# A two-layer encoder trunk on one core: block products in the FFN's input projection

## The chip, the core and the metric

The kernel runs on one core of a Trainium2 chip. The core has five engines that run their own instruction queues in order: TensorE (PE), which multiplies 128-row tiles and writes only to the accumulator memory PSUM; VectorE (DVE); ScalarE (ACT); GpSimd (POOL); and SyncE (SP), which here only issues DMAs. Data lie in SBUF, 128 partitions wide. The metric is device time in microseconds of one execution, as the median of several.

## The reference

Input x is 256 tokens by 1024. Two layers, each with three residual sub-layers; all is float32. The FFN is the part that the change touches:

```python
def _swiglu(h, w_in, w_out):
    gate, up = jnp.split(h @ w_in, 2, axis=-1)      # w_in 1024 x 5632
    return (jax.nn.silu(gate) * up) @ w_out         # w_out 2816 x 1024

for l in range(2):
    h = _swiglu(_rmsnorm(x, g[0]), ffn_w_in[l, 0], ffn_w_out[l, 0])
    x = x + 0.5 * _rmsnorm(h, g[1])
    h = _mixer(_rmsnorm(x, g[2]), ...)              # attention heads and mLSTM heads
    x = x + _rmsnorm(h, g[3])
    h = _swiglu(_rmsnorm(x, g[4]), ffn_w_in[l, 1], ffn_w_out[l, 1])
    x = x + 0.5 * _rmsnorm(h, g[5])
```

## The kernel before

**Six phases** follow one another: FFN, mixer, FFN, FFN, mixer, FFN. There are two token tiles of 128 (t = 0, 1), and the dimension D = 1024 is cut into two halves (kh = 0, 1) of four blocks of 128 each (k).

**Precision in two parts.** Matmuls run on a rounded float32 form, so each operand is split into a high part and a low remainder, and each block product is three matmuls into the same PSUM bank: high by high, high by low, low by high (`mm3`, L401 to L403). Tokens are the stationary operand (128x128), weights the moving one (128x512).

**Weights** come as pieces of 1 MB (128 x 2048): `begin_piece` issues the DMA on SP's queue into one of three raw buffers (`wr`), and each of its two halves (128 x 1024) is cast to its high part on ACT (L288, `wh`) and subtracted to its low part on DVE (L289, `wl`). The halves live in two pools of seven (`wl`, `wh`); while `lend` is set, three halves of every ten are taken from a third pool (`k4`, six tiles, two for each half). The cast and the split of a half wait until an older half has been used up by PE.

**An FFN phase** goes over the 2816 hidden columns in 11 chunks of 256 (gate and up, so 512 columns of w_in). For a chunk, two pieces of w_in are used: `in_piece` makes 12 matmuls for each token tile and half of D, 48 in all, into one bank for each token tile (tags `pin` and `ptr`, two banks each, in turns). `ffn_hidden` then makes silu(gate) * up: an ACT instruction (`func`, L266) and one on DVE (L528). `ffn_planes` turns the result: ACT copies it to 16-bit planes (L535), a transposing DMA on SP's queue follows (L537), DVE copies it back to float32 (L539, `hT`), and `ffn_hilo` splits it (L550 on ACT, L551 on DVE) into four buffers of each of `hh` and `hl`, two chunks' worth. `out_part` multiplies that by a piece of w_out (24 matmuls for both token tiles) into four banks that stay for the phase (`bk`). The output projection of a chunk runs behind the input projection of a later one (`DEFER`). The last chunk (`in_turned`, L610 and L615, `ffn_turned`) computes the transposed product directly, so that it needs no transposing DMA, and the outputs of chunks 8, 9 and 10 come last, token tile 0 ahead of 1, so that the norms of the next phase can begin. The first FFN phase starts with a chunk of its own, written out by hand (`first_chunk`), in which L371 splits the first two pieces.

**Around a phase**, `postnorm` and `prenorm_half` scale, add, transpose (L427) and split the tokens (L431 to L433) into tiles with the tag `both`, four buffers: two for the tokens of a phase, two more that the mixer uses for its output.

**Order.** Instructions are written in program order, and a scheduler that simulates the engines when the program is built fixes each engine's order and gives out buffers as they come free in its simulation. Only around the ends of phases (from "ending" to "running") is PE's order that of the program. `turns` and `after` add single orderings by hand. Small tiles of 128 x 512 (`h`, `planes`, `turned`, `hT` and others) share five buffers by the tag `ev`.

Of the kernel before, what the change touches and what calls it, by code (L numbers as in the profile page):

```python
# [17 lines left out]
F32 = mybir.dt.float32  # L18
F32R = mybir.dt.float32r
# [6 lines left out]
P = 128  # L26
# [10 lines left out]
DEFER = 3  # L37
TURN = 10
# [21 lines left out]
def _pack(inp):  # L60
# [9 lines left out]
    def ffn(at, l, f):  # L70
        a = w_in[l, f].reshape(2, 4, P, 2, NC_FF, 256)
        a = a.transpose(4, 0, 2, 1, 3, 5).reshape(NC_FF, 2, P, 2048)
        b = w_out[l, f].reshape(NC_FF, 2, P, D).transpose(0, 2, 1, 3).reshape(NC_FF, P, 2048)
        order = [a[0, 0], a[0, 1]]
        for c in range(1, NC_FF):
            order += [a[c, 0], a[c, 1], b[c - 1]]
        for piece in order + [b[NC_FF - 1]]:
            w[at] = piece
            at += 1
# [52 lines left out]
class _Trunk:  # L132
# [16 lines left out]
    for _n in ("nat", "ra", "rb", "rv", "tmp", "y", "so", "xg", "h", "planes", "turned", "hT"):  # L149
        TAGS[_n] = ("ev", 5)  # L150
# [32 lines left out]
    def constants_mix(self):  # L183
# [53 lines left out]
        self.qk = self.ded.tile([P, 4, S], F32, name="qk")  # L237
        self.qd = self.ded.tile([P, 2, CH], F32, name="qd")
        self.vx = self.ded.tile([P, NT, 4, P + 1], F32, name="vx")
        self.wt = self.ded.tile([P, NT, 2, 2, P], F32, name="wt")  # L240
# [36 lines left out]
    def begin_piece(self):  # L277

        nc, i = self.nc, self.piece_at
# [3 lines left out]
        js = iter(range(2))  # L283

        def part():
            j = next(js)
            lo, hi = self.half_tiles(i, j)
            ia = nc.scalar.activation(hi, raw[:, j], AF.Copy)  # L288
            iv = nc.vector.tensor_tensor(lo, raw[:, j], hi.bitcast(F32), op=ALU.subtract)  # L289
            for oa, ov in self.turns.pop(0) if self.turns else ():  # L290
                self.after(ia, [oa] if oa else [])
                self.after(iv, [ov] if ov else [])
            return hi, lo

        return part

    def half_tiles(self, i, j):
# [3 lines left out]
        return [pools[n].tile([P, 1024], F32R, tag=pools[n + 1], name=f"{nm}_{i}_{j}") for n, nm in ((0, "wl"), (2, "wh"))]  # L301
# [31 lines left out]
    def first_chunk(self, pins, xT):  # L333
# [30 lines left out]
        def H(i, k):  # L364
            if k % 2 == 0:
                lo[i, k // 2], hi[i, k // 2] = self.half_tiles(i, k // 2)
            self.cast = nc.scalar.activation(self.cols({k // 2: (hi[i, k // 2], lo[i, k // 2])}, k)[0], raw(i, k), AF.Copy)
# [162 lines left out]
    def ffn_planes(self, h):  # L530


        nc = self.nc
        planes = self.t2("planes", (P, 2, 512), U16)
        nc.scalar.activation(planes, h.rearrange("p t j -> p (t j)").bitcast(U16).rearrange("p (n u) -> p u n", u=2), AF.Copy)  # L535
# [3 lines left out]
        nc.vector.tensor_copy(hT.rearrange("p b n -> p (b n)").bitcast(U16).rearrange("p (n u) -> p u n", u=2),  # L539
                              turned.rearrange("p (u b) n -> p u (b n)", u=2))  # L540
        ops = [self.ffn_operand() for _ in range(NT)]
        for t in range(NT):
            self.ffn_hilo(hT[:, 2 * t:2 * t + 2], *ops[t])
        return [[tuple(v[:, k] for v in ops[t]) for k in range(2)] for t in range(NT)]
# [42 lines left out]
    def ffn(self, pre, gi_post):  # L587
# [30 lines left out]
        po, pend = None, []  # L618
        if not xT:
# [12 lines left out]
            h = self.t2("h", (P, NT, 256))  # L632
            for t in range(NT):
                self.ffn_hidden(pins[t], r[t], h[:, t])
            h = self.ffn_planes(h)
            begin = 1
        else:
# [17 lines left out]
            pend = [(0, self.ffn_planes(h), self.piece())]  # L655
# [6 lines left out]
            h = self.ffn_planes(h)  # L662
            begin = 2
        for c in range(begin, NC_FF):
            ws = [self.piece(), self.piece()]
            pend.append((c - 1, h, self.piece()))
            if c == 3:
                g = self.load_gpost(gi_post)
                yield "middle"
            if c < TURN:  # L670
                pins = [self.bank_pin() if c % 2 else self.bank_tr() for _ in range(NT)]
# [3 lines left out]
                h = self.t2("h", (P, NT, 256))  # L675
                for t in range(NT):
                    self.ffn_hidden(pins[t], r[t], h[:, t])
                h = self.ffn_planes(h)
            else:
                rows, both = self.token_scales(r), list(self.both)  # L680
                banks = [[self.bank_pin() for _ in range(2)], [self.bank_tr() for _ in range(2)]]
                in_turned(banks, ws, both)
                break
            if len(pend) == DEFER - 1:
                if po is None:
                    po = [[self.bank_bk() for _ in range(2)] for _ in range(NT)]
                cc, hc, wo = pend.pop(0)
                for t in range(NT):
                    out_part(cc, t, hc, wo)

        yield "ending"
        pend.append((c, self.ffn_turned(banks, rows), self.piece()))
        for p in pend:
            out_part(p[0], 0, *p[1:])
        yield "done", po[0], g
        for p in pend[:-1]:
            out_part(p[0], 1, *p[1:])
        yield "next"
        out_part(pend[-1][0], 1, *pend[-1][1:])
# [58 lines left out]
class _Mixer:  # L758


    def __init__(self, tr, pre, l):
        self.tr, self.l = tr, l
        self.xT, self.r = pre
        self.yT = [[None, None] for _ in range(NT)]
        self.conved = None
        self.rot, self.qkT, self.so, self.p = [], [], [], {}
        self.aT, self.lsum, self.hn, self.y = [None] * NT, [None] * NT, [None] * NT, [None] * NT
# [145 lines left out]
    def conv_silu(self):  # L913
        tr, conv = self.tr, self.conved
        tr.func(tr.qk, conv, AF.Silu)
        self.q, self.kT = tr.qk[:, 0:2, :], tr.qk[:, 2:4, :]
# [119 lines left out]
    def intra_weights(self):  # L1036
# [9 lines left out]
        for t in range(NT):  # L1046
            for hh in range(2):
                eE = self.eE[t].rearrange("p (a b j) -> p a b j", a=2, b=2)
                self.stt(tr.wt[:, t, :, hh, :], pss[hh][:, t], 0.125, eE[:, :, hh, :], op0=ALU.mult, op1=ALU.mult)
# [116 lines left out]
    def numerators(self, t):  # L1166
# [3 lines left out]
        for pr in range(2):  # L1170
            for hh in range(2):
                mm(num[hh][:, pr, :], tr.wt[:, t, pr, hh, :], tr.vx[:, t, 2 * pr + hh, :],
# [84 lines left out]
```

## Time and profile before

| | us |
|---|---|
| median of 3 runs | 961.61 (961.54 to 962.01) |
| the profiled execution | 962.02 |
| its span | 960.2 |
| PE, ACT, DVE busy | 952.8, 571.2, 638.7 |
| first FFN phase, until the next norm's first transposes | 0 to 185 |
| first mixer | 185 to 293 |
| FFN phases two and three | 293 to 477 to 659 |
| second mixer, last FFN | 659 to 766 to 960 |

The bounds of the phases are the starts of the prenorm's transposes on PE (L427) in the chain that ended last. A few per cent of the matmul records can be missing. In a row of a group stand the line, engine, operation, output and inputs by name, how many, then busy time in all and the mean of one in ns, then the idle time of the engine just before them and what released it. A row of windows has the stretch, then for PE, PEld (weight loads), DVE, ACT and POOL the busy time with the count, then the clock, the DMA share and GB/s; with a line given it has only that line's engine. A row of the timeline has start, length, engine, line, operation and, where several were merged, their count. The length of a matmul in the trace is more than the time until the next one starts, as matmuls are pipelined.

### The profile page before, as it was taken

To read this page: it belongs to the slowest core of one execution; us is meant where nothing else is said; L and a number is where in the kernel's file an instruction comes from. 1 tells how busy PE (TensorE), PEld (TensorE's weight loads), DVE (VectorE), ACT (ScalarE), POOL (GpSimd) and SP (SyncE) were. 2 spreads that over 40 slices of the span, in tenths; PEclk is the share of its full clock that TensorE was granted. 3 is DMA by queue.
4 is the path that set the end of the run, shared out by engine and by line. 5 is a ranking of instruction groups with operands and counts; after the bars stand their busy time and mean duration, and the time that the engine had idled before them with its cause. 6 is when DMAs were issued, how large, how long until landed. Compare 5 with 4: busy or idle time off the path is not lost.

```text
span 960.2 us, 12037 instructions
## 1 busy us (share of the span) xinstructions
PE 952.8 (99%) x4523; PEld 788.9 (82%) x4523; DVE 638.7 (67%) x945; ACT 571.2 (59%) x937; POOL 29.5 (3%) x55
## 2 busy tenths in 40 slices
PE   9999999999999999999999999999999999999997
PEld 7888888888888888888888888888888888888885
DVE  6765655689867766555687555566988676755553
ACT  8755554577856655454476555555778466555542
POOL 2000000000010000000000000000001000000000
PEclk9999999999999999999999999999999999999999
DMA  8996656236352975676458666653454257765621
GB/s 317 328 288 202 225 193 219 105 132 241 116 192 91 299 245 193 218 247 176 154 189 283 206 225 208 196 187 128 172 202 174 90 182 256 272 205 192 225 72 44
DMA packets 69879, 189.32 MB, mean 197 GB/s; under 512 B 45274, under 2 KB 46426, under 8 KB 49086
## 3 DMA queue, kind: packets, MB, share of 16 engines
q1 hardware_dynamic: 69246, 187.95, 58.0%
q8 instruction: 35, 0.57, 0.2%
q10 hardware_dynamic: 576, 0.61, 0.2%
q14 instruction: 22, 0.18, 0.1%
HBM read 177.01 MB, written 1.05 MB: 185 GB/s over the span
## 4 chain that ended last, share of the span: by engine, by line
PE 97%; DVE 1%; DMA 1%; ACT 0%; issue 0%; POOLq 0%; DVEq 0%; ACTq 0%
PE pin L401 13%; PE pin L402 13%; PE pin L403 13%; PE bk L401 10%; PE bk L402 10%; PE bk L403 10%; PE ptr L402 6%; PE ptr L403 6%; PE ptr L401 6%; PE pin L610 1%; PE ptr L610 1%; PE ptr L879 1%; PE ptr L427 1%; DMA wr<-in_w_dram 1%; PE bk L1094 1%; PE ptr L615 1%
## 5 line engine op out<-in xcount | busy, mean ns | idle before, releaser
L289 DVE TENSOR_TENSOR wl<-wr,wh 128x1024 fp32r<-128x1024 f32 x324 | 389.2, 1221 | 180.4 <-ACT wh L288 174.4
L288 ACT ACTIVATE wh<-wr 128x1024 fp32r<-128x1024 f32 x324 | 333.9, 1055 | 171.2 <-DMA wr<-in_w_dram 44.1
L401 PE MATMUL pin<-wh,both 128*128 128x512 f32 x560 | 221.2, 396 | 0.0
L403 PE MATMUL pin<-wh,both 128*128 128x512 f32 x560 | 218.3, 390 | 0.0
L402 PE MATMUL pin<-wl,both 128*128 128x512 f32 x560 | 218.2, 390 | 0.0
L401 PE MATMUL bk<-wh,hh 128*128 128x512 f32 x352 | 137.4, 390 | 0.1
L402 PE MATMUL bk<-wl,hh 128*128 128x512 f32 x352 | 137.0, 389 | 0.0
L403 PE MATMUL bk<-wh,hl 128*128 128x512 f32 x352 | 136.9, 389 | 0.0
L403 PEld LDWEIGHTS pin<-wh,both 128*128 128x128 f32 x560 | 105.1, 188 | 22.3
L401 PEld LDWEIGHTS pin<-wh,both 128*128 128x128 f32 x560 | 105.3, 188 | 22.0 <-issue 0.7
L402 PEld LDWEIGHTS pin<-wl,both 128*128 128x128 f32 x560 | 105.3, 188 | 20.6
L403 PE MATMUL ptr<-wh,both 128*128 128x512 f32 x256 | 99.4, 389 | 0.0
L402 PE MATMUL ptr<-wl,both 128*128 128x512 f32 x256 | 99.4, 389 | 0.0
L401 PE MATMUL ptr<-wh,both 128*128 128x512 f32 x256 | 98.9, 389 | 0.0
L401 PEld LDWEIGHTS bk<-wh,hh 128*128 128x128 f32 x352 | 66.1, 188 | 14.0 <-ACT hh L550 0.5
L403 PEld LDWEIGHTS bk<-wh,hl 128*128 128x128 f32 x352 | 66.1, 188 | 13.7
L402 PEld LDWEIGHTS bk<-wl,hh 128*128 128x128 f32 x352 | 66.1, 188 | 13.5
L539 DVE COPY hT<-turned 128x1024 uint16<-128x1024 uint16 x40 | 30.3, 757 | 41.9 <-DMA turned<-planes 41.5
L401 PEld LDWEIGHTS ptr<-wh,both 128*128 128x128 f32 x256 | 48.1, 188 | 10.0
L402 PEld LDWEIGHTS ptr<-wl,both 128*128 128x128 f32 x256 | 48.1, 188 | 10.0
L550 ACT ACTIVATE hh<-hT 128x256 fp32r<-128x256 f32 x80 | 28.9, 409 | 46.0 <-DVE hT L539 46.0
L403 PEld LDWEIGHTS ptr<-wh,both 128*128 128x128 f32 x256 | 48.1, 188 | 9.9
(210 smaller groups left out, 891.9 us busy)
## 6 DMA issues: line engine op xcount, KB each, us to landing
wr<-in_w_dram SPq DMA_DIRECT2D x162, 1024.0 KB, 5.2
gpost<-in_gpost_dram SPq DMA_DIRECT2D x6, 512.0 KB, 6.3
wr<-in_w_dram SPq DMA_DIRECT2D x2, 512.0 KB, 6.1
wr<-in_w_dram SPq DMA_DIRECT2D x3, 256.0 KB, 4.3
x<-in_x_dram SPq DMA_DIRECT2D x3, 256.0 KB, 4.4
turned<-planes SPq DMA_TRANSPOSE x40, 4.4
out_dram<-x SPq DMA_DIRECT2D x2, 256.0 KB, 2.1
x<-in_x_dram SPq DMA_DIRECT2D x2, 128.0 KB, 3.0
```

The costliest lines, as they stand in the source:

```text
L288: ia = nc.scalar.activation(hi, raw[:, j], AF.Copy)
L289: iv = nc.vector.tensor_tensor(lo, raw[:, j], hi.bitcast(F32), op=ALU.subtract)
L401: mm(ps, xh, wh, start=start, stop=False)
L402: mm(ps, xh, wl, start=False, stop=False)
L403: mm(ps, xl, wh, start=False, stop=stop)
L427: nc.tensor.transpose(ptr[:, k, :], x[:, (4 * hf + k) * P:(4 * hf + k + 1) * P], self.ident)
L539: nc.vector.tensor_copy(hT.rearrange("p b n -> p (b n)").bitcast(U16).rearrange("p (n u) -> p u n", u=2), turned.rearrange("p (u b) n -> p ...
L550: self.nc.scalar.activation(hh, h, AF.Copy)
L610: self.nc.tensor.matmul(b, self.cols(w[kh], k)[0][:, c], both[kh][:, k].rearrange("p i t -> p (i t)"), start=kh == 0 and k == 0, stop=Fals ...
L615: self.nc.tensor.matmul(b[:, 0:NT * P], self.cols(w[kh], k)[1][:, c], both[kh][:, k, 0:NT].rearrange("p i t -> p (i t)"), start=False, sto ...
L879: self.T(ptr[:, b, :], a[:, b * P:(b + 1) * P], self.tr.ident)
L1094: self.mm(pcs[c][:, h, :], self.qkT[0][rows, h0 + h, t * P:(t + 1) * P], self.qkT[1][rows, h0 + h, 0:nk], start=True, stop=True)
```

## The change

Write the tokens as four blocks X(kh, t) and the weights of two neighbouring chunks as four blocks W(kh, g), where g is gate or up, now for both chunks at once (512 columns each). Each of the four results (t, g) is a sum over kh of two block products, eight in all. Strassen's form in Winograd's arrangement gets them from seven products (P1 to P7) of sums of blocks. In each FFN phase chunks 4, 5 and chunks 8, 9 are done so.

- The phase is a list of steps (`STEPS`): I for a chunk's input projection as before, P for a pair, O for a chunk's output projection. The pieces in memory follow that order; a pair has four pieces, one for each block.
- `pair_tokens` makes, once a phase, four sums of token blocks from their high and low parts, and splits them again, into two more `both` tiles.
- `pair_blocks` splits seven blocks of weights in place of four: three blocks as loaded (P1, P2, P3) and four sums, which take four additions of whole blocks (128 x 2048, in two DVE instructions each). Three of the sums follow one another in a tile of their own (`wide`), the fourth lies in the raw buffer of its operand.
- `pair` runs the seven products into four banks, where P2, P3 and P4 accumulate on the bank of an earlier one, and adds the rest with DVE in tiles u, v and h0 of 512 columns.
- For all chunks the copy `hT` after the transposing DMA goes from DVE to ACT.
- The mixer's tiles `qk` and `wt` lie in the `wide` tile, which the mixer takes while no pair uses it.

```diff
-DEFER = 3
-TURN = 10
+STEPS = "I2 O0 I3 O1 P4 O2 I6 O3 I7 O4 O5 P8 O6 O7 I10".split()
+END = (8, 9, 10)
...
+    def fetch(self):
+        nc, i = self.nc, self.piece_at
+        self.piece_at += 1
+        raw = self.raw_tile(i)
+        self.load = nc.sync.dma_start(raw.rearrange("p a b -> p (a b)"), self.a["w"][i])
+        return raw
+
+    def halved(self, raw):
+        nc = self.nc
+        lo, hi = self.half_tiles()
+        ia = nc.scalar.activation(hi, raw, AF.Copy)
+        iv = nc.vector.tensor_tensor(lo, raw, hi.bitcast(F32), op=ALU.subtract)
...
+        return hi, lo
+
+    def wide(self):
+        return self.k4.tile([P, 2, 1024], F32, tag="wide", bufs=1, name=self.name("wide"))
+
+    def pair_blocks(self):
+        def split(raw):
+            return [self.halved(raw[:, j]) for j in range(2)]
+
+        def add(out, a, b):
+            for j in range(2):
+                self.nc.vector.tensor_tensor(out[:, j], a[:, j], b[:, j], op=ALU.add)
+
+        b11, b12 = self.fetch(), self.fetch()
+        w = {"P1": split(b11)}
+        run = self.wide()
+        add(run, b11, b12)
+        w["P5"] = split(run)
+        b22 = self.fetch()
+        add(run, run, b22)
+        w["P6"] = split(run)
+        add(b12, b12, b22)
+        w["P7"] = split(b12)
+        b21 = self.fetch()
+        w["P2"] = split(b21)
+        w["P3"] = split(b22)
+        add(run, run, b21)
+        w["P4"] = split(run)
+        return w
+
+    def pair_tokens(self, both):
+        tt = self.nc.vector.tensor_tensor
+        tiles = [self.tr.tile([P, 4, 2 * NT, P], F32R, tag="both", name=self.name("both")) for _ in range(2)]
...
+        s1 = apart((0, 1), (1, 1))
+        x1 = split(0, s1)
+        s2 = less((0, 0), s1)
+        x2 = split(1, s2)
+        x4 = split(3, less((1, 0), s2))
+        return x1, x2, split(2, apart((0, 0), (0, 1))), x4
...
         nc.sync.dma_start_transpose(turned, planes.rearrange("p u n -> p (u n)"))
-        hT = self.t2("hT", (P, 4, P))
-        nc.vector.tensor_copy(hT.rearrange("p b n -> p (b n)").bitcast(U16).rearrange("p (n u) -> p u n", u=2),
-                              turned.rearrange("p (u b) n -> p u (b n)", u=2))
+        hT = self.t2("hT", (P, 2, 2, P))
+        nc.scalar.activation(hT.rearrange("p a b n -> p (a b n)").bitcast(U16).rearrange("p (n u) -> p u n", u=2),
+                             turned.rearrange("p (u b) n -> p u (b n)", u=2), AF.Copy)
+        return hT
...
+        def product(b, x, w, new):
+            for k in range(4):
+                for n, (st, mv) in enumerate(((x[0], 0), (x[0], 1), (x[1], 0))):
+                    self.nc.tensor.matmul(b, st[:, k, :], self.cols(w, k)[mv], start=new and k == n == 0,
+                                          stop=k == 3 and n == 2, skip_group_check=True)
+
+        def pair(c):
+            tt, stt = self.nc.vector.tensor_tensor, self.nc.vector.scalar_tensor_tensor
+            w = self.pair_blocks()
+            b1, b2, b3, b4 = self.bank_pin(), self.bank_pin(), self.bank_tr(), self.bank_tr()
+            s1, s2, s3, s4 = sums
+            product(b1, xT[0][0], w["P1"], True)
+            p1 = self.t2("p1")
+            self.nc.scalar.activation(p1, b1, AF.Copy)
+            product(b4, s1, w["P5"], True)
+            product(b2, s2, w["P6"], True)
+            u, v, h0, sil = self.t2("u"), self.t2("v"), self.t2("h"), self.t2("sil")
+            tt(u, b2, p1, op=ALU.subtract)
+            product(b3, s3, w["P7"], True)
+            tt(v, u, b3, op=ALU.subtract)
+            tt(v, v, b4, op=ALU.add)
+            product(b1, xT[0][1], w["P2"], False)
+            self.func(sil, b1, AF.Silu, scale=r[0])
+            product(b4, s4, w["P3"], False)
+            tt(h0, b4, u, op=ALU.add)
+            stt(h0, h0, r[0], sil, op0=ALU.mult, op1=ALU.mult)
+            hT = [self.ffn_planes(h0)]
+            product(b3, xT[1][1], w["P4"], False)
+            tt(u, b3, u, op=ALU.subtract)
+            self.func(u, u, AF.Silu, scale=r[1])
+            stt(v, v, r[1], u, op0=ALU.mult, op1=ALU.mult)
+            hT.append(self.ffn_planes(v))
+            for j in range(2):
+                hs[c + j] = self.ffn_split([h[:, j] for h in hT])
```

Here `apart` is three DVE instructions of 512 columns, `less` two, and the `split` of tokens one on ACT and one on DVE, as `ffn_hilo`. The steps of the list are then run in its order, and the outputs of chunks 8, 9 and 10 come last as before.

More of the change, by code (lines that the diff above doesn't have):

```diff
@@ L148 @@
     TAGS = {"kwn": ("kwn", 1), "aT0": ("aT0", 1), "aT1": ("aT1", 1)}
-    for _n in ("nat", "ra", "rb", "rv", "tmp", "y", "so", "xg", "h", "planes", "turned", "hT"):
+    for _n in ("nat", "ra", "rb", "rv", "tmp", "y", "so", "xg", "h", "planes", "turned", "hT", "u", "v", "sum"):
         TAGS[_n] = ("ev", 5)
@@ L277, in begin_piece @@
     def begin_piece(self):
+        raw, js = self.fetch(), iter(range(2))
+        return lambda: self.halved(raw[:, next(js)])
+    def fetch(self):
         nc, i = self.nc, self.piece_at
@@ new lines, in pair_tokens, with a, apart, less @@
+    def pair_tokens(self, both):
+        tt = self.nc.vector.tensor_tensor
+        tiles = [self.tr.tile([P, 4, 2 * NT, P], F32R, tag="both", name=self.name("both")) for _ in range(2)]
+        def a(kh, t, lo):
+            return both[kh][:, :, lo * NT + t, :].bitcast(F32)
+        def apart(x, y):
+            s, low = (self.t2("sum", (P, 4, P)) for _ in range(2))
+            tt(s, a(*x, 0), a(*y, 0), op=ALU.subtract)
+            tt(low, a(*x, 1), a(*y, 1), op=ALU.subtract)
+            tt(s, s, low, op=ALU.add)
+            return s
+        def less(x, y):
+            s = self.t2("sum", (P, 4, P))
+            tt(s, a(*x, 0), y, op=ALU.subtract)
+            tt(s, s, a(*x, 1), op=ALU.add)
+            return s
+        def split(i, s):
+            hi, lo = (tiles[i // 2][:, :, n + i % 2, :] for n in (0, NT))
+            self.ffn_hilo(s, hi, lo)
+            return hi, lo
+        s1 = apart((0, 1), (1, 1))
[4 more added lines that the diff above has]
+        return x1, x2, split(2, apart((0, 0), (0, 1))), x4
@@ L631, in ffn @@
                 r.append(self.rsqrt_sum(ss, EPS))
[L632 to L636, printed above, removed]
+            chunk(0, pins)
+            w1 = [self.piece(), self.piece()]
+            pins = [self.bank_pin() for _ in range(NT)]
+            for kh in range(2):
+                for t in range(NT):
+                    in_piece(t, kh, pins[t], w1[kh])
+            chunk(1, pins)
         else:
@@ L661, in ffn @@
             self.ffn_hidden(pb1, r[1], h[:, 1])
[L662 to L671, printed above, removed]
+            hs[1] = ready(h)
+        both, sums, swap = list(self.both), None, 0
+        for step in STEPS[:-1]:
+            c = int(step[1:])
+            if step[0] == "P":
+                sums = sums or self.pair_tokens(both)
+                pair(c)
+            elif step[0] == "I":
+                if c == 3:
+                    g = self.load_gpost(gi_post)
+                    yield "middle"
+                ws = [self.piece(), self.piece()]
+                pins = [self.bank_pin() if swap else self.bank_tr() for _ in range(NT)]
+                swap = 1 - swap
                 for kh in range(2):
@@ L674, in ffn @@
                         in_piece(t, kh, pins[t], ws[kh])
[L675 to L689 removed]
+                chunk(c, pins)
+            else:
+                if not po:
+                    po = [[self.bank_bk() for _ in range(2)] for _ in range(NT)]
+                wo = self.piece()
+                for t in range(NT):
+                    out_part(c, t, hs[c], wo)
+        ws = [self.piece(), self.piece()]
+        rows = self.token_scales(r)
+        last = [self.piece() for _ in END[:-1]]
+        banks = [[self.bank_pin() for _ in range(2)], [self.bank_tr() for _ in range(2)]]
+        in_turned(banks, ws, both)
         yield "ending"
[L692 to L694 removed]
+        hs[END[-1]] = self.ffn_turned(banks, rows)
+        last.append(self.piece())
+        for c, wo in zip(END, last):
+            out_part(c, 0, hs[c], wo)
         yield "done", po[0], g
[L696 to L697 removed]
+        for c, wo in zip(END[:-1], last):
+            out_part(c, 1, hs[c], wo)
         yield "next"
[L699 removed]
+        out_part(END[-1], 1, hs[END[-1]], last[-1])
         yield "done", po[1], g
```

69 lines of the change are left out of this document (38 added, 31 removed).

## The prediction

> **What bounds the kernel now.** I read the page's busy table first, then the cost of one matmul from stretches of the trace, then who waits for whom.
>
> ```profile
> PE 952.8 (99%) x4523; PEld 788.9 (82%) x4523; DVE 638.7 (67%) x945; ACT 571.2 (59%) x937; POOL 29.5 (3%) x55
> L289 DVE TENSOR_TENSOR wl<-wr,wh 128x1024 fp32r<-128x1024 f32 x324 | 389.2, 1221 | 180.4 <-ACT wh L288 174.4
> L288 ACT ACTIVATE wh<-wr 128x1024 fp32r<-128x1024 f32 x324 | 333.9, 1055 | 171.2 <-DMA wr<-in_w_dram 44.1
> 500.00:630.00 130.00, 130.00 (x575) 107.70 (x574) 79.38 (x95) 73.83 (x95) 0.00 (x0) 1.00 0.68 223
> 321.72 1.06 ACT L288 ACTIVATE wh<-wr 128x1024 fp32r<-128x1024 f32 x1 [1.66 <-PE pin L402]
> ```
>
> TensorE (PE) is busy for 99% of the span. The row of the stretch from 500 to 630 us, inside one FFN phase, has the busy time of PE, weight loads, VectorE (DVE), ScalarE (ACT) and POOL, then the clock, the DMA share and GB/s: 575 matmuls in 130.0 us, so one starts every 0.2261 us, at clock 1.00 and without a gap. DVE is busy for 79.4 of these 130 us (61%). Its largest work is the split of weights (L289, the low half), which idles 180 us for the high half from ACT (L288), and the last row shows why ACT itself waits: for PE to give a buffer back. The weights are made ahead of PE until the buffers are full. So in the FFN phases PE alone sets the time, and DVE has a lead of some halves of a piece.
>
> A rule of the Trainium skill (Perfetto Trace Analysis, Identifying the Most-Contended Engine) speaks against this reading: matmul busy time says little, since matmuls are pipelined, and the busy share of LDWEIGHTS is a better measure. Here that share is 82%. By the 0.188 us of a weight load, 96 matmuls fewer would be worth 18.0 us; by the distance between starts they are worth 21.7 us. The stretch above has no gap between starts, so I go by the second.
>
> **What the change removes.** A pair of chunks took 2 chunks x 2 token tiles x 2 halves of D x 4 x 3 = 96 matmuls of 512 columns, and takes 7 x 4 x 3 = 84. Two pairs in each of four FFN phases: 96 fewer, 96 x 0.2261 = 21.7 us. The profiled execution took 962.0 us, its span 960.2; were nothing else to change, it would be 940.3. All other PE work stays, in another order.
>
> **What it adds.** The rows for its prices are these (start, length, instruction; "x6" is six merged).
>
> ```profile
> 308.39 6.90 DVE L289 TENSOR_TENSOR wl<-wr,wh 128x1024 fp32r<-128x1024 f32 x6 [0.25 <-ACT wh L288]
> 305.47 1.28 DVE L431 TENSOR_TENSOR xg<-ptr,c 128x512 f32<-128x512 f32 x2
> 300.66 1.42 DVE L481 SCALAR_TENSOR_TENSOR x<-tmp,rs,x 128x512 f32<-128x512 f32 x2
> 324.35 0.76 DVE L551 TENSOR_TENSOR hl<-hT,hh 128x256 fp32r<-128x256 f32 x2
> L528 DVE SCALAR_TENSOR_TENSOR h<-pin,rs,sil 128x256 f32<-128x256 f32 x46 | 22.0, 479 | 10.8 <-ACT sil L266 10.8
> L539 DVE COPY hT<-turned 128x1024 uint16<-128x1024 uint16 x40 | 30.3, 757 | 41.9 <-DMA turned<-planes 41.5
> L535 ACT ACTIVATE planes<-h 128x1024 uint16<-128x1024 uint16 x40 | 42.1, 1052 | 8.6 <-DVE h L528 8.4
> L550 ACT ACTIVATE hh<-hT 128x256 fp32r<-128x256 f32 x80 | 28.9, 409 | 46.0 <-DVE hT L539 46.0
> L266 ACT ACTIVATE sil<-pin,rs 128x256 f32<-128x256 f32 x46 | 21.5, 468 | 24.1 <-PE pin L403 20.3 <-POOL rs L416 3.8
> ```
>
> DVE instructions overlap by some 0.09 us, so back to back they cost less than their length: a split 1.14 us (6.90 less one of 1.22, over five), an operation of 512 columns 0.60, one with a scalar 0.67, one of 256 columns 0.34, h (L528) 0.39, the copy hT 0.66. The addition of two half blocks of weights (128x1024) isn't in the trace. L289 has its shape and both operands in SBUF: between 1.14 and its full 1.22; I take 1.14, since these additions stand in a busy queue.
>
> - A **pair on DVE**: 14 splits and 8 additions of weights (25.1), u, v twice, h0 and the last u (5 x 0.60 = 3.0), two with a scalar (1.3), four hl (1.4): 30.8 us, where PE needs 84 x 0.2261 = 19.0. Before, two chunks cost 8 splits, 4 h, 4 hl and 2 hT: 13.4.
> - **Sums of tokens**, once a phase: 10 operations and 4 low halves of 512 columns: 8.4 us.
> - **hT** leaves DVE (40 x 0.66 = 26) for ACT, at about 1.05 as L535 (nearest form): +42 us on ACT, and ACT, not DVE, now waits the 41.5 us for the transposing DMA.
>
> DVE's busy time goes from 639 to about 639 + 8 x 17.4 + 4 x 8.4 - 24 x 0.66 = 796 us, or 84% of 945. In the stretch from the third chunk to the last product before the turned chunk, DVE has four chunks at 6.0 us, eight output pieces at 2.27, two pairs and the sums, 112 us, against PE's 4 x 10.85 + 8 x 5.43 + 2 x 19.0 = 124.8. So the average still fits (90%), and the question is the **lead** where a pair asks for 30.8 us of DVE in 19.0 of PE. ACT has some 98 us of work in that stretch (8 chunks at 9.1, which are six casts, two sil, two hh and planes by the rows above; 12 more casts at 1.06, 8 hT, and 4 for the small ones): 78%, and 85% with its wait for transposes (1.04 each). It isn't the bound, but DVE waits behind it.
>
> **The lead at the first pair** (I2 O0 I3 O1 P4 O2).
>
> ```profile
> 0.00:317.20 317.20, 127.69 (x107) 1.00 0.60 207
> 316.54 2.36 DVE L289 TENSOR_TENSOR wl<-wr,wh 128x1024 fp32r<-128x1024 f32 x2 [0.85 <-ACT wh L288]
> 320.10 1.23 DVE L289 TENSOR_TENSOR wl<-wr,wh 128x1024 fp32r<-128x1024 f32 x1 [1.19 <-ACT wh L288]
> ```
>
> The first row counts the splits of L289 up to 317.2 us: 107. The second FFN phase begins with the 95th (98 halves come before it, four of which are split by L371). The third row brings one more by 321.3, with the second of the pair in the row above. PE is done with chunks 0 and 1 at about 321.4, which used eight: about seven halves of lead. From then until PE may begin O2, DVE owes 21 splits and 8 additions (33.1), the sums (8.4), u and v (1.8), h0 (1.3) and three chunks' hidden work (3.7): 48.3 us. PE has 2 x 10.85 + 2 x 5.43 + 19.0 = 51.6. DVE suffices as long as it is busy for 94% of that time; at a share e, PE waits 48.3/e - 51.6.
>
> What e can be:
>
> ```profile
> 206.00:236.00 30.00, 30.00 (x141) 24.76 (x141) 29.53 (x52) 24.39 (x33) 0.00 (x0) 1.00 0.52 194
> 306.00:318.00 12.00, 12.00 (x55) 9.92 (x54) 10.79 (x13) 9.94 (x13) 0.00 (x0) 1.00 0.63 239
> ```
>
> In the mixer DVE is busy for 29.5 of 30 us (98%), with ACT at 81%; while it fills the weight buffers after a norm, 10.8 of 12 (90%). I take e = 0.93, between the two; for the ends I take 1.0 and 0.85, as far below the lower row as a chain of addition, ACT cast and split through a queue in order might cost. At 0.93 PE waits 0.3 us in each of phases two to four.
>
> **The first phase** starts with less:
>
> ```profile
> 18.60:29.50 10.90, 7.17 (x7) 1.00 0.95 232
> 40.30:62.00 21.70, 11.53 (x10) 1.00 1.00 328
> 27.61 2.36 DVE L289 TENSOR_TENSOR wl<-wr,wh 128x1024 fp32r<-128x1024 f32 x2 [3.10 <-ACT wh L288]
> 50.94 0.42 DVE L212 TENSOR_TENSOR lamp<-lamv 128x256 f32<-128x256 f32 x1 [4.40 <-DMA lamv<-in_lam_dram]
> ```
>
> DMA is at a share of 0.95 to 1.00 up to 62 us, and when chunk 2 begins (29.5) eight halves are made since the first chunk, four of them chunk 1's: a lead of four. That is 3.4 us more to do, the constants and an hl 1.9, and DVE stands 4.4 us before lamp. Against that, the 3.1 us it idled before 27.6 can take some of the sums. So 50.5 to 58, and I take the middle, 54: at 0.93 it is 58.1 - 51.6 = 6.5 us of waiting.
>
> **The second pair** is covered: between O2 and P8, PE has 4 x 5.43 + 2 x 10.85 = 43.4 us, and DVE owes 24 splits, 6 additions and 5.5 of hidden work, 39.7, with the fourth product's weights not due until 8.1 us into the pair.
>
> **The wait that is added.** P3 accumulates in the bank of P5, so its first matmul waits until DVE has read P7 and P5 into v. Behind P7 PE still has P2, 12 x 0.2261 = 2.71 us; DVE needs 2 x 0.60, plus 1.14 for each split that stands ahead. With one ahead it fits (2.34), with two it is 0.8 late. What is queued behind the waiting matmul is all of P3 and P4, and if v stands too early in DVE's queue, all splits behind it wait. Between nothing and 0.8 I take 0.25 each, 2 us for eight pairs.
>
> The raw pieces stay at four a pair. A pair holds the three raw buffers longer: the fourth block loads once the first is added (4.5 us of DVE after the start; a load takes 5.2 us by the page's DMA issues), and is due after 15.9 us of DVE work. It is hidden; a late load would cost lead, which is in e. The transposes and the loads share SP's queue, and go from one to two transposes per pair of chunks' tokens, the same number as before (40).
>
> ```profile
> wr<-in_w_dram SPq DMA_DIRECT2D x162, 1024.0 KB, 5.2
> turned<-planes SPq DMA_TRANSPOSE x40, 4.4
> ```
>
> **Sum**: 962.0 - 21.7 + 6.5 + 3 x 0.3 + 2 = 949.7. The median of the runs shown, 961.6, is 0.4 below the profiled run: 949.3.
>
> **Rivals.**
>
> 1. *All of it hidden.* With e near 1 and the sums in the first phase's idle time, no wait is left but the second's bound of v: 940 to 943, at 941. For it: the mixer's 98%. Against it: the first phase's thin lead.
> 2. *DVE's queue becomes the bound, and it is slower than before.* The place is the first pair of each phase, the price 54/e - 51.6 in the first and 48.3/e - 51.6 in the other three, plus 2. At e = 0.88 that is 9.8 + 3 x 3.3 + 2 = 21.7, which is all that was saved: the deciding point. At 0.85: 11.9 + 15.7 + 2 = 29.6, or 969.5. For it: 38.1 us of waiting in 27 pieces, below, in a stretch where DVE had little to do; half of such waits kept would bring e there. Against it: these waits have full buffers behind them, as the ACT row of 321.72 shows.
> 3. *The gain is just cancelled*, e of 0.87 to 0.89: 960 to 964.
> 4. *The clock falls after a wait.* The first matmuls, behind an idle start, take longer than later ones:
>
> ```profile
> DVE wl L289 <- ACT wh L288: 38.1, 27, 3.3
> 0.76 3.04 PE L390 MATMUL bk<-const-bfloat16-1.0 128*128 128x512 bf16 x9 [0.76 <-PEq L1247]
> L390 PE MATMUL bk<-const-bfloat16-1.0 128*128 128x512 bf16 x8 | 3.9, 617 | 0.8 <-PEq L1247 0.8
> L403 PE MATMUL pin<-wh,both 128*128 128x512 f32 x560 | 218.3, 390 | 0.0
> ```
>
> 617 against 390 ns, and 9 matmuls (some narrower) in 3.04 us, about half the later rate, until some 6 us; the granted clock reads 1.00 all the same. If a wait of PE brought that back, each would cost up to half of 5.4 us. With 2.7 for each of four first pairs the forecast becomes 960. The Trainium skill (TensorE: Matmul & The Clock Gate, HAM oscillation — how this bites in real kernels) states that an idle gap over about 3.4 us brings the slow clock back. The trace of before has no such gap, so no row here bears it out. My waits come in pieces of one split, 1.14 to 2.3 us, so this is unlikely unless rival 2 holds.
> 5. *The change doesn't save the matmuls* (a count of PE instructions that stays at 4523): same time. The diff shows seven products, so this is small.
>
> **Chances.** Forecast 0.46 (own range 943 to 957), rival 1 0.26, rival 2 0.14, rival 3 0.07, rival 4 0.05, rival 5 0.02. The range 940 to 963 holds all but rival 2, and little more. About 0.2% is what a measurement of this kernel can tell from no change: faster 0.46 + 0.26 + 0.02 (rival 4) = 0.74; same 0.07 + 0.03 + 0.02 = 0.12; slower 0.14.
>
> **What would show it.** PE instructions down by 96 to about 4427, and still 0.226 us apart inside products. Idle time of PE, now 7 us in the span, up to about 17, most of it in the first phase, at weight loads released by L289's successor on DVE. DVE at 84%, with additions of about 1.2 us in length. DVE's 41.5 us before hT turned into ACT's. P3 waiting for v by under 1 us. Wrong would be: PE's idle time near zero (rival 1), over 29 us (rival 2), or spread evenly over both pairs, which would mean that the ledger of the lead has the wrong place.

## The result, and the profile after

The changed kernel takes 988.49 us (986.47 to 991.07, four runs) against 961.81 (961.54 to 962.8, four runs of the kernel before on the same chip): a ratio of 1.0277 [1.0245, 1.0309]. It is slower by 2.8%, where 949.3 us was predicted. The profiled execution took 990.41 us, its span 988.6, which is 28.4 more than before.

First the busy table of the changed kernel's page and two of its groups, in the columns of the rows shown of before.

```profile
PE 950.4 (96%) x4427; PEld 778.7 (79%) x4427; DVE 788.2 (80%) x1097; ACT 669.5 (68%) x1033; POOL 29.3 (3%) x55
L297 DVE TENSOR_TENSOR wl<-wr,wh 128x1024 fp32r<-128x1024 f32 x324 | 386.6, 1219 | 69.4 <-ACT wh L296 68.6
L609 ACT ACTIVATE hT<-turned 128x1024 uint16<-128x1024 uint16 x40 | 54.9, 1373 | 56.7 <-DMA turned<-planes 56.5
```

PE has 96 instructions fewer (4523 to 4427): the matmuls are gone. But PE's busy time fell by only 2.4 us instead of 21.7, and its idle time rose from 7.4 to 38.2 us (span less busy). So the 28.4 us are -21.7 (matmuls) + 30.8 (idle) + 19.3: the matmuls that stayed were busy for 19.3 us longer. The wait of DVE's split for ACT fell from 174.4 to 68.6 us, so the lead in weights is used up far more.

Where it is, the windows of the changed kernel show (stretch, then PE, PEld, DVE, ACT and POOL busy with counts, granted clock, DMA share, GB/s). The first four rows lie around the first pair of each phase, the last three at the ends of the first three FFN phases.

```profile
60.00:90.00 30.00, 23.12 (x82) 17.59 (x81) 29.88 (x37) 19.82 (x24) 0.00 (x0) 0.83 0.43 149
360.00:400.00 40.00, 35.15 (x144) 27.37 (x143) 35.96 (x42) 25.01 (x30) 0.00 (x0) 0.96 0.48 164
550.00:590.00 40.00, 33.01 (x128) 25.06 (x127) 33.41 (x41) 23.55 (x29) 0.00 (x0) 0.91 0.45 157
850.00:870.00 20.00, 14.86 (x57) 11.14 (x56) 19.02 (x25) 12.71 (x18) 0.00 (x0) 0.92 0.55 171
180.00:190.00 10.00, 7.51 (x25) 5.36 (x25) 6.39 (x16) 4.83 (x14) 0.00 (x0) 0.83 0.35 126
480.00:490.00 10.00, 7.76 (x26) 5.67 (x25) 5.81 (x15) 4.73 (x13) 0.00 (x0) 0.83 0.50 197
670.00:680.00 10.00, 9.47 (x45) 7.55 (x44) 7.55 (x19) 6.23 (x16) 0.00 (x0) 1.00 0.60 211
```

Stretch less PE's busy time is PE's idle time: 6.9, 4.9, 7.0 and 5.1, together 23.9 us at the four first pairs, and 5.3 at the ends; that is 29.1 of the 38.2. The clock is at 1.00 in the rows of before that the prediction quotes; here it is down to 0.83. Length times (1 - clock) is about what a lower clock took: 11.9 us at the first pairs, 3.4 at the ends, 15.3 of the 19.3. So the **first pairs** cost some 36 us and the **ends** some 9. With the 7.4 us of idle time that were there before, 1.7 are left for all the rest, the second pairs' products among it.

The view of PE's waits says for whom (total, times, longest):

```profile
PE pin L705 <- ACT p L717: 9.1, 4, 3.1
PE ptr L705 <- ACT both L624: 7.5, 4, 2.5
PE ptr L705 <- DVE both L625: 3.9, 3, 1.6
```

These are the three largest, all before the pairs' products (L705), and they come four or three times, about once a phase: for the copy p1 of the first product, and for the high and low halves of a sum of **tokens** (`both`). None of them is for weights. The order of PE at the first pair of the third phase, in its timeline:

```profile
560.50 0.50 PE L705 MATMUL pin<-wh,both 128*128 128x512 f32 x1 [2.02 <-ACT p L717]
565.57 0.50 PE L705 MATMUL ptr<-wh,both 128*128 128x512 f32 x1 [2.06 <-ACT both L624]
567.53 1.22 PE L705 MATMUL ptr<-wh,both 128*128 128x512 f32 x2 [1.23 <-DVE both L625]
571.11 0.63 PE L705 MATMUL ptr<-wl,both 128*128 128x512 f32 x1
571.54 0.63 PE L705 MATMUL ptr<-wh,both 128*128 128x512 f32 x1
```

P2 (with weights and tokens as loaded) follows right behind P1 instead of P5, and must wait for p1 to leave the bank that it adds to. Then P5 waits for the first sum of tokens, whose making begins with this row of DVE's timeline, beside the copy hT of chunk 3, the last chunk before the pair, in ACT's:

```profile
561.33 0.69 DVE L344 TENSOR_TENSOR sum<-both,both 128x512 f32<-128x512 f32 x1
```

```profile
561.93 1.37 ACT L609 ACTIVATE hT<-turned 128x1024 uint16<-128x1024 uint16 x1 [1.49 <-DMA turned<-planes]
```

The tokens (`both`) are there from the start of a phase. The first of DVE's 14 operations on the sums starts only at 561.33, when PE has done the pair's first product and is at P2. Behind the three waits, matmuls start 0.43 us apart (571.11 to 571.54) instead of 0.23: the clock.

### The profile page after: what moved, and what is told of

Its sections match the earlier page's. It is cut to its first block, busy times and chain, and to the rows that moved or that the text cites. A ratio compares the mean times of both kernels' runs of the same rounds, so it can differ in the third digit from the quotient of the medians.

```text
span 988.6 us, 12155 instructions
## 1 busy us (share of the span) xinstructions
PE 950.4 (96%) x4427; PEld 778.7 (79%) x4427; DVE 788.2 (80%) x1097; ACT 669.5 (68%) x1033; POOL 29.3 (3%) x55
## 3 DMA queue, kind: packets, MB, share of 16 engines
HBM read 177.01 MB, written 1.05 MB: 180 GB/s over the span
## 4 chain that ended last, share of the span: by engine, by line
PE 73%; DVE 10%; ACT 8%; DMA 6%; issue 3%; SPq 0%; POOLq 0%; DVEq 0%; ACTq 0%
PE ptr L705 9%; PE bk L473 8%; PE bk L472 8%; PE bk L471 8%; PE pin L471 8%; PE pin L473 8%; PE pin L472 8%; PE pin L705 5%; DVE wl L297 5%; DMA turned<-planes 4%; ACT wh L296 3%; DMA wr<-in_w_dram 2%; PE ptr L471 2%; PE ptr L472 2%; PE ptr L473 2%
## 5 line engine op out<-in xcount | busy, mean ns | idle before, releaser
L297 DVE TENSOR_TENSOR wl<-wr,wh 128x1024 fp32r<-128x1024 f32 x324 | 386.6, 1219 | 69.4 <-ACT wh L296 68.6
L471 PE MATMUL pin<-wh,both 128*128 128x512 f32 x432 | 171.3, 398 | 0.0
L473 PE MATMUL pin<-wh,both 128*128 128x512 f32 x432 | 168.4, 390 | 0.0
L472 PE MATMUL pin<-wl,both 128*128 128x512 f32 x432 | 168.4, 390 | 0.0
L705 PE MATMUL ptr<-wh,both 128*128 128x512 f32 x256 | 88.9, 411 | 11.4 <-ACT both L624 7.5
L473 PEld LDWEIGHTS pin<-wh,both 128*128 128x128 f32 x432 | 81.1, 188 | 17.4
L471 PEld LDWEIGHTS pin<-wh,both 128*128 128x128 f32 x432 | 81.3, 188 | 17.0 <-issue 0.7
L472 PEld LDWEIGHTS pin<-wl,both 128*128 128x128 f32 x432 | 81.2, 188 | 15.5
L609 ACT ACTIVATE hT<-turned 128x1024 uint16<-128x1024 uint16 x40 | 54.9, 1373 | 56.7 <-DMA turned<-planes 56.5
L705 PE MATMUL pin<-wh,both 128*128 128x512 f32 x192 | 66.7, 409 | 10.2 <-ACT p L717 9.1
L705 PEld LDWEIGHTS ptr<-wh,both 128*128 128x128 f32 x256 | 50.2, 197 | 25.5 <-ACT both L624 9.2
L297 DVE TENSOR_TENSOR wl<-wide,wh 128x1024 fp32r<-128x1024 f32 x48 | 57.7, 1217 | 2.5 <-ACT wh L296 2.1
L296 ACT ACTIVATE wh<-wide 128x1024 fp32r<-128x1024 f32 x48 | 49.4, 1049 | 13.3 <-DVE wide L314 8.0
L625 DVE TENSOR_TENSOR hl<-hT,hh 128x256 fp32r<-128x256 f32 x80 | 30.9, 418 | 32.8 <-ACT hh L624 32.8
L705 PEld LDWEIGHTS pin<-wh,both 128*128 128x128 f32 x192 | 38.1, 199 | 21.0 <-ACT p L717 10.8
```

Of the source, the lines that this page charges most:

```text
L296: ia = nc.scalar.activation(hi, raw, AF.Copy)
L297: iv = nc.vector.tensor_tensor(lo, raw, hi.bitcast(F32), op=ALU.subtract)
L471: mm(ps, xh, wh, start=start, stop=False)
L472: mm(ps, xh, wl, start=False, stop=False)
L473: mm(ps, xl, wh, start=False, stop=stop)
L609: nc.scalar.activation(hT.rearrange("p a b n -> p (a b n)").bitcast(U16).rearrange("p (n u) -> p u n", u=2), turned.rearrange("p (u b) n - ...
```

## The experiments

Each was profiled once and timed beside the kernel before on the same chip: 961.54 us for the first four below, 962.25 for the next four. The last three have intervals. The four runs of the changed kernel lie 4.6 us apart, so a few microseconds between single runs say little.

### Where the loss isn't: the order and the copy hT

```diff
-STEPS = "I2 O0 I3 O1 P4 O2 I6 O3 I7 O4 O5 P8 O6 O7 I10".split()
+STEPS = "I2 O0 I3 O1 I4 I5 O2 I6 O3 I7 O4 O5 I8 I9 O6 O7 I10".split()
```

> The changed kernel with chunks 4, 5, 8 and 9 computed one by one: 96 matmuls more, no sums of tokens, no additions of weights, but the new order of steps and hT on ACT. Theory (the loss arises in the pairs alone): 960 to 964 us, as before. Rival (the new order or hT on ACT loses time without pairs): above 968, with waits of PE at the ends of the FFN phases.

Measured 961.58 us, against 961.54. The new order and hT on ACT cost nothing by themselves. All of the loss comes with the pairs.

### Sums of tokens or additions of weights

```diff
-                sums = sums or self.pair_tokens(both)
+                sums = [xT[0][0], xT[1][1], xT[0][1], xT[1][0]]
```

> The products P5, P6, P7 and P3 take plain token blocks in place of their sums; the sums are left out (8.4 us of DVE in each phase). Theory (the sums of tokens stand too late in DVE's queue and the first pair waits for them): of some 38 us that PE loses around the four first pairs at most 12 stay, 955 to 965 us. Rival (the additions and splits of weights are what PE waits for there): at least 25 of the 38 stay, 975 or more.

Measured 953.47 us. (This kernel and the next leave out a part of the arithmetic, so they only serve to place the time.) The window of its first pair in the first phase, where the changed kernel lost most:

```profile
60.00:90.00 30.00, 30.00 (x134) 24.82 (x133) 28.79 (x31) 23.17 (x26) 0.00 (x0) 1.00 0.68 237
```

No idle time, the full clock, and 134 matmuls in place of 82. The other side of it keeps the sums and takes the additions of weights away:

```diff
-        add(run, b11, b12)
-        w["P5"] = split(run)
+        w["P5"] = split(b11)
...
-        add(run, run, b22)
-        w["P6"] = split(run)
-        add(b12, b12, b22)
+        w["P6"] = split(b22)
...
-        add(run, run, b21)
-        w["P4"] = split(run)
+        w["P4"] = split(b21)
```

> The four additions of weight blocks in each pair are left out, with the same 14 splits (9.1 us less of DVE in each pair, twice the sums' work in a phase). Theory (sums of tokens too late): they still come behind the third chunk's work, so at least 15 of the 38 us stay at the first pairs, 965 to 980 us. Rival (DVE's amount of work at the pair): the waits go with the work, 945 to 955 us.

Measured 979.61 us. Its busy table and one window:

```profile
PE 944.9 (97%) x4427; PEld 774.9 (79%) x4427; DVE 720.3 (74%) x1033; ACT 668.6 (68%) x1033; POOL 29.8 (3%) x55
```

```profile
60.00:90.00 30.00, 24.94 (x102) 19.71 (x101) 26.42 (x34) 19.56 (x24) 0.00 (x0) 0.94 0.47 163
```

DVE has 68 us less to do and the first pair still loses: 5.1 us idle at a clock of 0.94. In all, 9 of the 27 us are gone, while the sums, half as much work (34 us in four phases), took all 27 with them and more. So the amount of DVE's work, which my rival 2 would have had, is at most a part of it. The main cause is the 8 us of sums in each phase that arrive late. What makes them late was still open: their place in the program (they are written just ahead of the pair), or the buffers that they take.

### Place or buffers

The scratch of the sums is allocated by `t2`, so it shares the five buffers of the tag `ev` with h, planes, turned and hT of every chunk. Four combinations of early or late place and shared or own buffers tell the two apart; the changed kernel is late and shared. First both, early and own, in one kernel. Early is

```diff
-        both, sums, swap = list(self.both), None, 0
+        both, sums, swap = list(self.both), self.pair_tokens(list(self.both)), 0
...
-                sums = sums or self.pair_tokens(both)
```

and own buffers, in the tile that `pair_blocks` uses later, are

```diff
+        room = self.wide()
+        at = iter([room[:, i // 2, (i % 2) * 512:(i % 2) * 512 + 512].rearrange("p (k n) -> p k n", k=4) for i in (0, 1, 2, 3, 0, 1)])
+
         def apart(x, y):
-            s, low = (self.t2("sum", (P, 4, P)) for _ in range(2))
+            s, low = next(at), next(at)
...
         def less(x, y):
-            s = self.t2("sum", (P, 4, P))
+            s = next(at)
```

> The same arithmetic; the sums of tokens are made right after chunk 1, with the wide tile as their room in place of the five shared buffers. Theory (too late a place): they run where DVE has idle time, the first pairs lose 5 to 15 us in all instead of 38, 957 to 970 us. Rival (DVE has no time to give before the first pair, wherever the sums stand): 980 or more.

Measured 961.56 us, 27 below the changed kernel. Then each alone. The early place with shared buffers:

> The place of the sums alone: made right after chunk 1, in the five buffers that they share with h, planes, turned and hT. Theory (their place in program order sets when they get buffers and their turn): most of the gain of e5_early_own, 958 to 968 us. Rival (the shared buffers hold them up at either place): 975 or more.

Measured 989.17 us: nothing gained. The first and the last row of DVE's operations on the sums in the last phase, and one of PE's:

```profile
832.61 0.69 DVE L344 TENSOR_TENSOR sum<-both,both 128x512 f32<-128x512 f32 x1
...
861.19 0.70 DVE L625 TENSOR_TENSOR both<-sum,both 128x512 fp32r<-128x512 f32 x1
```

```profile
861.94 1.22 PE L705 MATMUL ptr<-wh,both 128*128 128x512 f32 x2 [4.83 <-DVE both L625]
```

The sums begin earlier, but 8 us of work is strung out over 29, and when the last is done, at 861.89, PE has waited 4.83 us for it. Own buffers, at the place of the change:

> The room alone: the sums stay at the first pair's place in program order, but lie in the wide tile. Theory (place): little gain, 978 to 990 us. Rival (the five shared buffers, given out in program order, are what holds the sums up until the third chunk's hT): with a room of their own they run in DVE's idle time, 958 to 968.

Measured 958.54 us, 30 below the changed kernel. Here my theory (the place) fell and its rival held. Windows of this kernel, and two rows of its DVE in the second phase:

```profile
60.00:90.00 30.00, 27.68 (x114) 22.13 (x113) 29.02 (x30) 20.38 (x23) 0.00 (x0) 0.94 0.56 197
360.00:400.00 40.00, 40.00 (x178) 33.15 (x177) 36.05 (x39) 29.16 (x33) 0.00 (x0) 1.00 0.71 252
329.00:350.00 21.00, 21.00 (x94) 17.41 (x93) 20.52 (x26) 14.63 (x21) 0.00 (x0) 1.00 0.76 252
```

```profile
318.43 0.69 DVE L347 TENSOR_TENSOR wide<-both,both 128x512 f32<-128x512 f32 x1
...
342.63 0.69 DVE L628 TENSOR_TENSOR both<-wide,both 128x512 fp32r<-128x512 f32 x1
```

The changed kernel in the last of these stretches:

```profile
329.00:350.00 21.00, 21.00 (x95) 17.38 (x94) 14.76 (x16) 16.33 (x21) 0.00 (x0) 1.00 0.92 331
```

With own buffers the sums are made between 318 and 343 us, in time that DVE otherwise spends waiting: it is busy for 20.5 of 21 us there, against 14.8 in the changed kernel, and PE is at 21.00 in both. The time was there; the sums could not take it. The first pair of the second phase (360 to 400) then loses nothing, and P5 runs right behind P1 again (PE's timeline has P1's last matmul at 367.02 and P5's first at 367.25). At either place own buffers gain some 28 to 30 us; with own buffers the early place gains nothing (961.56 against 958.54). Which of the tiles in the five buffers held the sums back at each moment, the runs don't show; that it is the buffers, they do.

### The ends of the phases

At the end of the second phase PE waits for the outputs of chunks 8 and 9 (`bk`, O8 and O9). PE's timeline of the changed kernel:

```profile
483.04 0.50 PE L471 MATMUL bk<-wh,hh 128*128 128x512 f32 x1 [1.53 <-ACT hh L624]
484.48 0.75 PE L473 MATMUL bk<-wh,hl 128*128 128x512 f32 x1 [0.71 <-DVE hl L625]
```

What hh waits for, on ACT and on DVE:

```profile
472.03 1.38 ACT L609 ACTIVATE hT<-turned 128x1024 uint16<-128x1024 uint16 x1 [2.69 <-DMA turned<-planes]
473.27 1.03 ACT L605 ACTIVATE planes<-v 128x1024 uint16<-128x1024 uint16 x1
482.27 1.03 ACT L624 ACTIVATE hh<-hT 128x256 fp32r<-128x256 f32 x3
```

```profile
467.22 0.74 DVE L734 SCALAR_TENSOR_TENSOR v<-v,rs,u 128x512 f32<-128x512 f32 x1
```

v is ready at 467.96, but its planes stand on ACT behind the first hT, which waits 2.69 us for its transposing DMA; they begin at 473.27, 5.3 us after v, and the high half of hT (hh) that O8 and O9 need is made only from 482.27. Two experiments: hT back on DVE, and both transposes issued ahead of either copy back.

```diff
-        nc.scalar.activation(hT.rearrange(...), turned.rearrange(...), AF.Copy)
+        nc.vector.tensor_copy(hT.rearrange(...), turned.rearrange(...))
```

> The copy hT is on DVE again (26 us more of DVE, 55 less of ACT), all else as changed. Theory (at the ends of the FFN phases ACT stands before hT for the transposing DMA, and the second pair's last planes stand behind it): the 10 us lost at the ends fall to 3 or less; at the first pairs DVE loses about 2 us a phase more: 980 to 990 in all. Rival (the ends wait for the late weights and not for hT): the ends lose as much as before, 990 to 1000.

Measured 997.41 us, worse by 9, in the rival's range. The end of its second phase, in a window, and the copy on DVE and the planes of v on ACT:

```profile
480.00:500.00 20.00, 17.85 (x81) 14.35 (x80) 13.76 (x29) 11.27 (x25) 0.03 (x1) 0.91 0.80 220
```

```profile
484.48 0.77 DVE L609 COPY hT<-turned 128x1024 uint16<-128x1024 uint16 x1 [1.90 <-DMA turned<-planes]
```

```profile
482.49 1.05 ACT L605 ACTIVATE planes<-v 128x1024 uint16<-128x1024 uint16 x1
```

The theory that ACT's waiting copy alone makes the end late fell: with the copy on DVE the wait goes there, and the end loses as much as before (2.2 us idle). But the planes no longer stand behind a copy: v itself is ready only at 481.05 (DVE's timeline: 480.30 and 0.75 long), 1.4 us ahead of its planes and 13 later than in the changed kernel. That late weights make it so, as the rival has it, isn't shown. The order of issue is the other way:

```diff
-            hT = [self.ffn_planes(h0)]
+            hT = [self.ffn_turn(h0)]
...
-            hT.append(self.ffn_planes(v))
+            hT = [self.ffn_back(i) for i in hT + [self.ffn_turn(v)]]
```

(`ffn_turn` is `ffn_planes` up to the transposing DMA, `ffn_back` the copy hT.)

> In a pair both transposes are issued before either copy hT, so that the planes of v no longer stand behind the first hT on ACT. Theory (as for e7): the ends lose 4 us or less in all instead of 10, 980 to 984. Rival (late weights): no change, 986 to 991.

Measured 982.21 us, 6 below the changed kernel and below the lowest of its runs (986.47). Its window at the end of the second phase, and two rows of ACT:

```profile
480.00:490.00 10.00, 9.64 (x43) 7.34 (x42) 5.13 (x13) 2.79 (x9) 0.55 (x1) 1.00 0.31 106
```

```profile
466.10 1.05 ACT L608 ACTIVATE planes<-v 128x1024 uint16<-128x1024 uint16 x1
467.96 1.37 ACT L617 ACTIVATE hT<-turned 128x1024 uint16<-128x1024 uint16 x1 [0.81 <-DMA turned<-planes]
```

v's planes now run ahead of the first copy back, which waits 0.81 us instead of 2.69. The end loses 0.4 us of PE instead of 2.2, at the full clock.

### Both mended

Own buffers and the later copies back in one kernel:

> The wide tile as the sums' room, and both transposes of a pair ahead of the copies hT. Theory (two separate losses: the sums held up by the shared buffers, the ends by v's planes behind hT): the gains add up, 958.5 less some 7 to 12 us, 946 to 952 us, faster than before. Rival (with the sums out of the way another order at the ends, or the splits and additions, take the gain): 955 or more.

Measured 956.22 us (955.47 to 959.91, four runs) against 962.82: a ratio of 0.9943 [0.9922, 0.9964]. That is 2 us below the one run of own buffers alone, less than its own runs differ, where the two gains together would have given 952: the rival's range held. The end of the first phase, in its window:

```profile
170.00:190.00 20.00, 15.95 (x65) 12.10 (x64) 13.35 (x27) 11.01 (x24) 0.57 (x1) 0.91 0.40 144
```

4.1 us idle at a clock of 0.91: with the first pair less late, the end of this phase comes out late again. (With own buffers alone PE idles 5.5 us in this stretch, in the changed kernel 2.5.) Two more changes, each on top of this kernel. The first takes the sums from DVE, to relieve the first pair of the first phase:

```diff
     def pair_tokens(self, both):
-        tt = self.nc.vector.tensor_tensor
+        tt = self.nc.gpsimd.tensor_tensor
```

> As c1_own_late, with the ten additions and subtractions of the token sums in each phase on POOL, so that DVE has some 6 us less to do before the first pair. Theory (DVE's work before the first pair still costs the first phase some 4 us): 1 to 5 us faster than c1_own_late. Rival (POOL's longer operations delay the sums, or slow DVE): slower than c1_own_late by 2 or more.

Measured 974.50 us (972.37 to 976.24), a ratio of 1.0124 [1.0106, 1.0142]. A stretch of it beside the sums on POOL, and five splits on DVE:

```profile
320.00:330.00 10.00, 7.63 (x34) 6.00 (x32) 10.00 (x7) 4.00 (x6) 9.22 (x6) 1.00 0.83 283
```

```profile
316.70 11.24 DVE L297 TENSOR_TENSOR wl<-wr,wh 128x1024 fp32r<-128x1024 f32 x5
```

Five splits take 11.24 us instead of five times 1.14: the splits are halved in speed while POOL works, and PE waits 2.4 us of these ten. The rival held. The second change moves the second pair ahead of one output:

```diff
-STEPS = "I2 O0 I3 O1 P4 O2 I6 O3 I7 O4 O5 P8 O6 O7 I10".split()
+STEPS = "I2 O0 I3 O1 P4 O2 I6 O3 I7 O4 P8 O5 O6 O7 I10".split()
```

> As c1_own_late, with the second pair one output step earlier (O4 P8 O5 O6 O7). Theory (the ends no longer wait once v's planes are issued early): no gain, within 3 us of c1_own_late, or slower, since the second pair has 5.4 us less of lead. Rival (the second pair's hidden values are still late at the ends): 3 us or more faster.

Measured **949.51 us** (948.41 to 953.03, four runs) against 962.82: a ratio of 0.9878 [0.9853, 0.9902]. It is faster than both kernels, 1.2% faster than the one before, and again the rival held: the second pair's hidden values had still been late. Its page and two windows, the end of the first phase and its first pair:

```profile
PE 932.5 (98%) x4427; PEld 770.8 (81%) x4427; DVE 786.3 (83%) x1097; ACT 666.6 (70%) x1033; POOL 31.3 (3%) x55
```

```profile
160.00:180.00 20.00, 20.00 (x105) 17.11 (x105) 13.97 (x26) 14.06 (x26) 0.00 (x0) 1.00 0.77 270
60.00:90.00 30.00, 25.84 (x113) 20.68 (x112) 29.87 (x31) 20.66 (x24) 0.00 (x0) 1.00 0.56 204
```

The end loses nothing; the first phase's first pair still has 4.2 us of waiting, with DVE at 29.9 of 30 (the two waits, of 2.08 and 2.07 us, are for splits of weights, L297). PE's busy time is 932.5, within 1.4 of the 931.1 that 96 matmuls less give (952.8 - 21.7), and its idle time 14.2 (span of 946.7 less busy). DVE does the same work as in the slow kernel.

## Why the prediction was wrong

- **The matmuls** were right: 4427 instructions, and busy time down by 20.3 of the 21.7 us where the clock stays up (the last experiment).
- **The prices** were right for DVE: 788 us busy, against 796. hT on ACT was mis-sized: 1.37 us each instead of 1.05, and ACT waits 56.5 us for transposes, not 41.5. The second mattered at the ends.
- **"The lead at the first pair" failed**, the step that carried the sum. It charged DVE with 48.3 us against PE's 51.6 and counted the sums' 8.4 as work that DVE does whenever it is free. It summed work and asked for a busy share; it did not ask when each piece may start. The sums have their size, but no room: they share five buffers with every chunk's hidden tiles, so they began when chunk 3 was through, and P2 and P5 waited for p1 and the sums. Forecast 6.5 + 3 x 0.3 us, measured 23.9 idle and 11.9 of clock. With own buffers the ledger comes out nearly: nothing lost at the first pair of the second phase (0.3 forecast), and in the first phase 2.3 us idle and 1.8 of clock (6.5 forecast).
- **The ends were missing.** "The second pair is covered" is true of its products, but I followed the pair only up to them. Its hidden values for chunks 8 and 9 pass two ACT copies and a DMA for each token tile, and the phase's last outputs wait for them. I named the work on ACT and its wait and then judged them by a share (85%); in an in-order queue what mattered was that v's planes stood behind a waiting copy. This cost 5.3 us idle and 3.4 of clock.
- **The wait of P3 for v** was forecast at 2 us in all. The view of waits has one, of 0.4 us, at a weight load (PEld, L705, for v of L723).
- **The clock**, rival 4, was put at nothing in the sum and took some 15 us in the windows above, half of the 28.4. (The other 4 of the 19.3 us of longer busy time aren't placed.) I gave it 0.05, since waits of 1.14 to 2.3 us seemed too short for it; they were not, and they came from another cause than rival 2's. Rival 2's sign and size (969.5) were nearer than the forecast, but its mechanism, too much work for DVE, isn't the main thing that happened: 68 us less of it left 18 of the 27 us, and with own buffers and all of the work none of the 27 is left.

Left open: why the gains of own buffers and of later copies back don't add in full at the end of the first phase, and what makes v late once hT is on DVE. The one try at the wait that remains at the first phase's first pair, the sums on POOL, made the kernel slower.

## What to carry to other kernels

A ledger of work against time says whether an engine can keep up; it doesn't say when a piece may start. For each added piece, also ask which buffers it needs and who holds them, and what stands ahead of it in each in-order queue up to its last consumer. When independent work comes out at the last moment although its engine idles before, look at its buffers before its place in the program: here own scratch gave 30 us, an earlier place nothing. And price a wait of PE above its own length: the slow clock behind the waits took some 15 us here, beside 29 us of waiting.

## What the runs showed of the hardware

**A wait of about 2 us can bring the slow clock, and need not.** The first and the last kernel of the section on both mends differ little at the first pair of the first phase, and in both PE waits there for the same time. First with own buffers and later copies back, then with P8 moved, each in PE's timeline:

```profile
75.62 0.79 PE L716 MATMUL pin<-wl,both 128*128 128x512 f32 x1 [2.09 <-DVE wl L297]
77.06 0.63 PE L716 MATMUL pin<-wl,both 128*128 128x512 f32 x1
77.49 1.05 PE L716 MATMUL pin<-wh,both 128*128 128x512 f32 x2
```

```profile
76.58 0.50 PE L716 MATMUL pin<-wl,both 128*128 128x512 f32 x1 [2.08 <-DVE wl L297]
77.39 0.40 PE L716 MATMUL pin<-wl,both 128*128 128x512 f32 x1
77.63 0.62 PE L716 MATMUL pin<-wh,both 128*128 128x512 f32 x2
```

After 2.09 us one runs at half pace (0.43 us from start to start) for some 3 us; after 2.08 us the other keeps its pace (0.24). In the changed kernel no wait of PE was longer than 3.1 us, and at the end of the second phase 1.53 and 0.71 us in a row were enough. The rule that the prediction cited, an idle gap over about 3.4 us (the Trainium skill, TensorE: Matmul & The Clock Gate, HAM oscillation — how this bites in real kernels), does not describe this; here the measurement decides. The same page (What's actually happening) says that the clock is set by a window of about 3.4 us that runs freely and doesn't start anew with a kernel. The traces agree: in each of the thirteen the clock changes only at whole steps of 3.41 us from its earlier changes. Two rows of windows of the changed kernel, cut at such changes:

```profile
71.55:74.97 3.42, 1.18 (x5) 0.66 (x5) 3.42 (x6) 2.15 (x3) 0.00 (x0) 1.00 0.70 206
74.97:81.79 6.82, 5.24 (x12) 3.64 (x12) 6.79 (x12) 2.33 (x4) 0.00 (x0) 0.50 0.49 204
```

A step in which PE is busy for 1.18 us is followed by two steps at half the clock. Over the thirteen traces, with a matmul counted as 0.23 us from its start, each of the 41 falls of the clock ahead of the kernels' ends comes behind a step with at least 2.03 us of idle time, and no full-clock step that is followed by another has more than 2.07. By that count the step ahead of the slow stretch in the first timeline above is idle for 2.21 us (71.85 to 75.27), the one that holds most of the wait in the second for 1.98 (74.73 to 78.14): so it matters how much of a wait falls into one step. No run here moved a wait on purpose. Another section of the page (A second HAM failure mode: psum-queue depth-cycling) says that frequent short idle times make the clock go back and forth; the windows at 0.83 to 0.96 agree.

**GpSimd additions halve DVE's splits.** The five splits above took 2.25 us each beside POOL's additions, against 1.14 alone. The Trainium skill (SBUF — State Buffer, SBUF: two separate sides) states that the two engines share a pair of ports under an exclusive lock, which a DVE operation with two SBUF inputs takes against a GpSimd operation that reads SBUF; the rows agree that the two hold each other up, and don't show how the ports are shared.
